# LayerNorm mean of the Conformer module taken from the convolved tiles in PSUM, squares summed by pairs

## The chip, the cores and the metric

The kernel runs on one core of a Trainium2 chip. The metric is the device time of one execution in microseconds (us), from the runs of the same program on the chip.

## What is computed

The reference is one inference step of a two-layer trunk for 512 prompt tokens and 8 sequences of 8 sample tokens (576 token columns in the kernel). Layer 0 is a Mamba-2/S5 mixer and an MLP, layer 1 a Conformer convolution module and an MLP. The change lies in the convolution module:

```python
def conformer_conv_module(xn, buf, w_pw1, b_pw1, w_dw, b_dw, ln_w, ln_b, w_pw2, b_pw2):
    h = xn @ w_pw1 + b_pw1
    h = h[..., :C_CH] * jax.nn.sigmoid(h[..., C_CH:])
    h, new_buf = causal_depthwise_conv(h, buf, w_dw, b_dw)
    h = jax.nn.silu(layer_norm(h, ln_w, ln_b))
    return h @ w_pw2 + b_pw2, new_buf
```

There are 1024 channels and 31 taps; `layer_norm` subtracts the mean over the channels and divides by the root of the mean square of what is left.

## The kernel before

Activations lie with channels on the 128 partitions and the 576 token columns in the free dimension, so 1024 channels are eight tiles, m = 0 to 7. A dense layer is `mm` (L226): the weights are split in `load` into a high and a low part (ScalarE writes `hi`, L211; VectorE writes `lo`, L212), and each output tile takes 48 matmuls of 288 columns. Two PSUM buffers named `mm` alternate.

`conformer` loops over m. In each turn two `mm` calls give the gate (`cs`) and the value (`ct`), VectorE takes both out of PSUM (L1167) and multiplies them into `hb`, the convolution's input with 30 columns of history in front (L1189). `dwconv` of tile m-1 is written one turn later. It works in one of three ways:

- Tiles in the list `PT` go through `dwconv_pe`: a ScalarE copy (`hp`), a write to DRAM and four reads back in another order (`hq`), 36 matmul calls (72 instructions) with prepared weights `dm` (L1308), a ScalarE copy (`ho`), four writes and a read (`hy`), and a ScalarE pass with the bias into `acc` (L1317).
- Tiles with `ND` = 30 take their first tap on ScalarE and 30 taps on VectorE, one instruction of 512 columns each (L1376).
- Tile 7 is split: `ND[7]` taps on VectorE, the rest on TensorE against diagonal weights, three matmuls of 512 columns a tap (L1374), added by L1380.

The sample columns of each tile add eight small VectorE instructions (L1341).

The LayerNorm's mean is not taken from the results. `tap_sums` (L1259) multiplies each `hb` by its 31 tap weights and sums over channels in two PSUM banks (`pt`). After tile 7 `neg_mean` copies them to SBUF (`pz`), writes them to DRAM (`pzd`), reads them back with each tap's row shifted by its tap (`pk`), and sums the rows with a matmul against -1/1024 (`mu`, L1282); a ScalarE copy gives `nmu` (L1283). Biases and sample histories are centred ahead of time by `dwconv_center` in the first MLP. Tile 7's prompt columns get the mean through a matmul into their own bank (L1363); tiles 0 to 6 get it by a VectorE addition (L1208). Then ScalarE squares each tile (L1211) and ten one-column matmul instructions a tile sum the squares over channels (L1216), 80 in all. `rstd_tok`, `bcast_tok`, a VectorE product and a Silu on ScalarE lead to the second dense layer `w_pw2`, again `mm`.

The order on each engine is set by a scheduler with a cost model, by program order and by the offsets `HP` and `HPC`. Each engine then works through its list in that order. All DMAs named here are issued on SyncE's queue.

Of the kernel before, what the change touches and what calls it, by code (L numbers as in the profile page):

```python
# [8 lines left out]
F32 = mybir.dt.float32  # L9
# [129 lines left out]
def h2(t):  # L139
    return t.rearrange("p (h n) -> p h n", h=2)  # L140


class Build:
# [182 lines left out]
    def _ffn(self, i, x):  # L326
# [33 lines left out]
        for q in range(4):  # L360
            if q == 3 and i == 1:
                for n in range(16):
                    down_half(n % 8, g, n // 8)
                    if n == 9 or n == 15:
                        self.final(x, n // 15)
                break
            gn = []
            for m in range(8):
                if q < 3:
                    gn.append(up(q * 8 + 8 + m))  # L370
                if q == 1 and i == 0:
                    self.dwconv_state(self.qp, m)
                    if m == 7:
                        self.dwconv_center()
                if q == 0 and i == 0:
                    self.ssm_state(self.qp, m)
                down(q, m, g)
            g = gn
# [773 lines left out]

    ND = [0, 30, 0, 0, 30, 0, 30, 14]

    NEV = 1
    ORD = [0, 1, 2, 3, 4, 5, 6, 7]
    SQ = "aaaaaaaa"
# [10 lines left out]

    PT = [0, 2, 3, 5]
    NDM = 5  # L1170

    def conformer(self, x):
        nc, I = self.nc, self.I
        with self.tc.tile_pool(name="q2", bufs=2) as q:
            act = [self.split_scaled(x[k], self.v("nm1", k), "fx", self.B) for k in range(8)]
            _, rB = self.rms(x, "rB1")
            acc, hbs = [], []
            ps31 = [self.bank("pt0"), self.bank("pt1", "sf")]
            for m in range(8):
                ps = self.mm(I["w_pw1"][8 + m], act)  # L1180
                s = self.t("cs", "t")
                self.evac(s, ps, rB, m < self.NEV)
                nc.scalar.activation(s, s, AF.Sigmoid, bias=self.v("bpw1", 8 + m))
                ps = self.mm(I["w_pw1"][m], act)
                t = self.t("ct", "t2")
# [8 lines left out]
                if m in self.PT:  # L1194
                    for g in range(4):
                        self.dwconv_mat(q, m, g)
                with self.hp(self.HP if m == 7 else 0):
                    self.tap_sums(q, m, hb, ps31)
                if m > 0:
                    self.dwconv(q, m - 1, hbs[m - 1], acc[m - 1])  # L1200
            nmu = self.neg_mean(q, ps31)
            self.dwconv(q, 7, hbs[7], acc[7], nmu)
            nmu = nmu[0]

            ts = self.bank("tsum")
            for n, k in enumerate(self.ORD):
                if k < 7:
                    nc.vector.tensor_tensor(acc[k], acc[k], nmu, op=ALU.add)  # L1208
                s = self.B("sq")
                if self.SQ[n] == "a":  # L1210
                    nc.scalar.activation(s, acc[k], AF.Square)  # L1211
                else:
                    nc.vector.tensor_tensor(s, acc[k], acc[k], op=ALU.mult)
                for c in (0, 4, 1, 2, 3):
                    m = min(128, NT - c * 128)
                    nc.tensor.matmul(ts[:m, c:c + 1], s[:, c * 128:c * 128 + m], self.ones[:, 0:1], start=n + c == 0, stop=(n, c) == (7, 3))  # L1216
            r = self.tp.tile([128, 5], F32, tag="r5", name="r5")
# [11 lines left out]
    def dwconv_init(self, q):  # L1229

        nc = self.nc
        self.wdh = q.tile([128, 248], F32R, tag="wdh", name="wdh")
        self.wdl = q.tile([128, 248], F32, tag="wdl", name="wdl")
        nc.scalar.activation(self.wdh, self.v("dww", 0, 248), AF.Copy)
        nc.vector.tensor_tensor(self.wdl, self.v("dww", 0, 248), self.wdh.bitcast(F32), op=ALU.subtract)
        self.ss = q.tile([128, 8, 64], F32, tag="ss", name="ss")
        self.bdc = q.tile([128, 8], F32, tag="bdc", name="bdc")
        self.neg = q.tile([128, 128], F32, tag="neg", name="neg")
        nc.gpsimd.memset(self.neg, -1.0 / 1024)
        self.pzd = self.dp.tile([31, 670], F32, tag="pzd", name="pzd")  # L1240
        tiles = lambda n, s: {m: self.dp.tile(s, F32, tag="%s%d" % (n, m), name="%s%d" % (n, m)) for m in self.PT}
        self.dd, self.de = tiles("dd", [128, 4, 136]), tiles("de", [128, 4, 128])
        self.dm = {}

    def dwconv_center(self):

        nc = self.nc
        s = self.tp.tile([128, NT], F32, tag="sa", name="s1", bufs=1)
        nc.vector.tensor_reduce(s[:, 0:64], self.ss.rearrange("p m t -> p t m"), axis=mybir.AxisListType.X, op=ALU.add)
        nc.vector.tensor_reduce(s[:, 64:65], self.v("bdw", 0, 8), axis=mybir.AxisListType.X, op=ALU.add)  # L1250
        ps = self.bank("cm")
        nc.tensor.matmul(ps[:, 0:65], self.neg, s[:, 0:65], start=True, stop=True)
        nc.vector.tensor_tensor(self.ss, self.ss, ps[:, 0:64].unsqueeze(1).broadcast_to([128, 8, 64]), op=ALU.add)
        nc.vector.tensor_tensor(self.bdc, self.v("bdw", 0, 8), ps[:, 64:65].broadcast_to([128, 8]), op=ALU.add)

    def tap_sums(self, q, m, hb, ps):

        for h in range(2):
            self.nc.tensor.matmul(ps[h][:31, 0:H], self.v("dww", m * 31, 31), hb[:, 30 + h * H:30 + h * H + H], start=m == 0, stop=m == 7)  # L1259

    def neg_mean(self, q, ps):

        nc = self.nc
        pz = q.tile([31, 670], F32, tag="pz", name="pz", bufs=1)
        pk = q.tile([31, NT], F32, tag="pk", name="pk", bufs=1)
        nc.gpsimd.memset(pz[:, 0:30], 0.0)
        nc.gpsimd.memset(pz[:, 542:670], 0.0)
        nc.gpsimd.memset(pk[:, NP:NT], 0.0)
        out = q.tile([128, NT], F32, tag="nmu", name="nmu", bufs=1)
        with self.hp():  # L1270
            nc.scalar.activation(pz[:, 30:30 + H], ps[0][:31, 0:H], AF.Copy)
            nc.scalar.activation(pz[:, 30 + H:542], ps[1][:31, 0:NP - H], AF.Copy)
            nc.scalar.activation(pz[:, 542:670].rearrange("p (b j) -> p b j", b=8)[:, :, 8:16],
                                 ps[1][:31, NP - H:H].rearrange("p (b j) -> p b j", b=8), AF.Copy)
            nc.sync.dma_start(self.pzd, pz)
            nc.scalar.activation(q.tile([31, 1], F32, tag="ld", name="ld", bufs=1), pz[:, 31:32], AF.Silu)
            d = self.pzd
            nc.sync.dma_start(pk[23:31, NP:NT], bass.AP(tensor=d.tensor, offset=d.offset + 23 * 671 + 520, ap=[[671, 8], [16, 8], [1, 8]]))
            nc.sync.dma_start(pk[:, 0:NP], bass.AP(tensor=d.tensor, offset=d.offset, ap=[[671, 31], [1, NP]]))
            mu = self.pm.tile([128, 2, 512], F32, tag="mm", name="mu")[:, :, :H]  # L1280
            for h, o, n in ((0, 0, H), (1, 0, NP - H), (1, NP - H, 64)):
                nc.tensor.matmul(mu[:, h, o:o + n], self.neg[:31], pk[:, h * H + o:h * H + o + n], start=True, stop=True)  # L1282
            nc.scalar.activation(h2(out), mu, AF.Copy)  # L1283
        return out, pk

# [6 lines left out]
    def dwconv_pe(self, q, m, hb, a):  # L1292
# [18 lines left out]
        with self.hp(self.HPC):  # L1311
# [4 lines left out]
            nc.sync.dma_start(y, self.de[m])  # L1316
            nc.scalar.activation(a[:, 0:NP].rearrange("p (n f) -> p f n", f=4), y, AF.Identity, bias=self.bdc[:, m:m + 1])  # L1317

# [13 lines left out]

    def dwconv(self, q, m, hb, a, nmu=None):

# [4 lines left out]
        for d in range(8):  # L1339
            src = an if d else self.ss[:, m].rearrange("p (b t) -> p b t", b=8)  # L1340
            nc.vector.scalar_tensor_tensor(an[:, :, d:8], hn[:, :, 0:8 - d], self.v("dww", m * 31 + 30 - d), src[:, :, d:8],  # L1341
                                           op0=ALU.mult, op1=ALU.add)
        if nmu is not None:
            nc.vector.tensor_tensor(a[:, NP:], a[:, NP:], nmu[0][:, NP:], op=ALU.add)
        if m in self.PT:
# [5 lines left out]
        k0 = 1 + self.ND[m]  # L1351
        nc.scalar.activation(ap, hb[:, 0:NP], AF.Identity, scale=w(0), bias=self.bdc[:, m:m + 1])
        pc = None
        if k0 < 31:
# [5 lines left out]
            pc = self.bank("pc", "sd" if m % 2 else "sf")  # L1360
            if nmu is not None:
                with self.hp(self.HPC):
                    nc.tensor.matmul(pc, self.neg[:31], nmu[1][:, 0:NP], start=True, stop=False)  # L1363
            for k in range(k0, 31, 4):
# [7 lines left out]
                for j in range(n):  # L1372
                    for i, (dd, h) in enumerate(((dh, hh), (dh, hl), (dl, hh))):
                        nc.tensor.matmul(pc, dd[:, j], h[:, k + j:k + j + NP], start=k + j == k0 and i == 0 and nmu is None, stop=k + j == 30 and i == 2)  # L1374
        for k in range(1, k0):
            nc.vector.scalar_tensor_tensor(ap, hb[:, k:k + NP], w(k), ap, op0=ALU.mult, op1=ALU.add)  # L1376
        if pc is None and nmu is not None:
            nc.vector.tensor_tensor(ap, ap, nmu[0][:, 0:NP], op=ALU.add)
        if pc is not None:
# [39 lines left out]
```

## Time and profile before

| | us |
|---|---|
| median of three runs | 1678.6 (1676.21 to 1682.48) |
| the profiled execution | 1674.24 |
| its span, first to last instruction | 1672.5 |
| TensorE busy | 1591.3 |
| VectorE busy | 1054.5 |
| ScalarE busy | 634.8 |

A profile page gives the busy time of each engine, a strip of 40 equal slices of the span, and the chain of work that ended last. In the strip a digit is the busy share of a slice in tenths; the line PEclk shows the clock that TensorE was granted, in tenths of full speed. Each slice is 41.8 us. In lists of the trace L numbers are lines of the kernel, PEld is TensorE's weight load, `out<-in` names the tiles, and xN says how many instructions a row holds.

### The profile page before, as it was taken

To read this page: it belongs to the slowest core of one execution; us is meant where nothing else is said; L and a number is where in the kernel's file an instruction comes from. 1 tells how busy PE (TensorE), PEld (TensorE's weight loads), DVE (VectorE), ACT (ScalarE), POOL (GpSimd) and SP (SyncE) were. 2 spreads that over 40 slices of the span, in tenths; PEclk is the share of its full clock that TensorE was granted. 3 is DMA by queue.
4 is the path that set the end of the run, shared out by engine and by line. 5 is a ranking of instruction groups with operands and counts; after the bars stand their busy time and mean duration, and the time that the engine had idled before them with its cause. 6 is when DMAs were issued, how large, how long until landed. Compare 5 with 4: busy or idle time off the path is not lost.

```text
span 1672.5 us, 28815 instructions
## 1 busy us (share of the span) xinstructions
PE 1591.3 (95%) x11833; PEld 1557.6 (93%) x11833; DVE 1054.5 (63%) x1796; ACT 634.8 (38%) x1081; POOL 4.7 (0%) x45
## 2 busy tenths in 40 slices
PE   7999889999998999999999999996799999999997
PEld 7999789989897999999999999995799999999996
DVE  7988899876647966754443557587454443444466
ACT  4244556675514333322222353223333222222244
POOL 0000000000000000000000000000000000000000
PEclk9999999999998999999999999997799999999998
DMA  6644457687766434432222245641022222222234
GB/s 197 180 109 132 131 172 197 197 267 220 251 234 188 94 97 129 154 127 78 87 77 88 78 146 148 189 107 30 25 77 77 89 76 89 85 81 88 78 127 132
DMA packets 149883, 214.43 MB, mean 128 GB/s; under 512 B 59034, under 2 KB 94874, under 8 KB 149752
## 3 DMA queue, kind: packets, MB, share of 16 engines
q1 hardware_dynamic: 146088, 211.28, 41.2%
q8 instruction: 93, 1.52, 0.4%
q10 hardware_dynamic: 3664, 1.32, 0.3%
q14 instruction: 38, 0.31, 0.1%
HBM read 181.22 MB, written 31.34 MB: 127 GB/s over the span
## 4 chain that ended last, share of the span: by engine, by line
PE 82%; DVE 7%; DMA 6%; ACT 2%; issue 1%; SPq 1%; ACTq 0%; DVEq 0%
PE mm L226 72%; PE pc L1308 2%; DVE lo L212 1%; DMA sg<-cumd 1%; DMA rl<-yad 1%; PE pc L1374 1%; PE tsum L1216 1%; PE bc L310 1%; DMA rl<-ybd 1%; DMA rl<-yg 1%; PE pt L1259 1%; DMA ud<-u 1%; PE s5s L600 1%; PE s5y L704 0%; PE s5y L705 0%
## 5 line engine op out<-in xcount | busy, mean ns | idle before, releaser
L211 ACT ACTIVATE hi<-raw 128x1024 fp32r<-128x1024 f32 x217 | 229.7, 1060 | 740.2 <-PE mm L226 685.6
L226 PE MATMUL mm<-fxh,hi 128*128 128x288 f32 x1920 | 418.2, 299 | 23.8 <-ACT hi L211 10.4
L212 DVE TENSOR_TENSOR lo<-raw,hi 128x1024 fp32r<-128x1024 f32 x217 | 264.8, 1221 | 259.0 <-ACT hi L211 257.5
L226 PE MATMUL mm<-fxh,lo 128*128 128x288 f32 x1920 | 417.4, 298 | 0.0
L226 PE MATMUL mm<-fxl,hi 128*128 128x288 f32 x1920 | 415.0, 298 | 0.0
L226 PEld LDWEIGHTS mm<-fxh,hi 128*128 128x128 f32 x1920 | 311.7, 190 | 26.7 <-ACT hi L211 12.7
L226 PEld LDWEIGHTS mm<-fxh,lo 128*128 128x128 f32 x1920 | 311.6, 190 | 1.8 <-issue 1.1
L226 PEld LDWEIGHTS mm<-fxl,hi 128*128 128x128 f32 x1920 | 311.9, 190 | 0.4
L226 PE MATMUL mm<-gh,hi 128*128 128x288 f32 x1024 | 230.0, 295 | 0.0
L226 PE MATMUL mm<-gh,lo 128*128 128x288 f32 x1024 | 229.4, 295 | 0.5 <-DVE lo L212 0.5
L226 PE MATMUL mm<-gl,hi 128*128 128x288 f32 x1024 | 229.5, 295 | 0.0
L226 PEld LDWEIGHTS mm<-gh,lo 128*128 128x128 f32 x1024 | 167.5, 188 | 0.8 <-DVE lo L212 0.8
L226 PEld LDWEIGHTS mm<-gl,hi 128*128 128x128 f32 x1024 | 167.9, 188 | 0.0
L226 PEld LDWEIGHTS mm<-gh,hi 128*128 128x128 f32 x1024 | 167.6, 188 | 0.0
L350 DVE TENSOR_TENSOR fft<-mm,r2B 128x576 f32<-128x576 f32 x56 | 42.4, 758 | 140.5 <-PE mm L226 140.5
L1376 DVE SCALAR_TENSOR_TENSOR acc<-hb,vec,acc 128x512 f32<-128x512 f32 x104 | 77.2, 748 | 1.3
L343 DVE TENSOR_TENSOR ffr<-ffr 128x576 f32<-128x576 f32 x64 | 48.5, 758 | 2.3 <-ACT gh L342 0.4
L344 DVE TENSOR_TENSOR gl<-ffr,gh 128x576 fp32r<-128x576 f32 x64 | 48.5, 758 | 2.1
L342 ACT ACTIVATE gh<-ffr 128x576 fp32r<-128x576 f32 x64 | 44.1, 689 | 2.0
L351 DVE TENSOR_TENSOR x<-x,fft 128x576 f32<-128x576 f32 x56 | 42.4, 758 | 1.8
L765 DVE SCALAR_TENSOR_TENSOR cvo<-xb,vh,cvo 128x600 f32<-128x600 f32 x48 | 40.0, 833 | 1.4 <-ACT cvo L763 1.4
L340 ACT ACTIVATE ffr<-mm 128x576 f32<-128x576 f32 x64 | 40.6, 634 | 0.0
(356 smaller groups left out, 1903.1 us busy)
## 6 DMA issues: line engine op xcount, KB each, us to landing
raw<-w_ff SPq DMA_DIRECT2D x136, 512.0 KB, 3.5
raw<-w_in SPq DMA_DIRECT2D x33, 512.0 KB, 3.7
raw<-w_pw SPq DMA_DIRECT2D x24, 512.0 KB, 3.6
dm<-dwm SPq DMA_DIRECT2D x16, 576.0 KB, 5.9
h<-ass SPq DMA_DIRECT2D x16, 512.0 KB, 4.7
raw<-w_out SPq DMA_DIRECT2D x16, 512.0 KB, 4.5
U<-ud SPq DMA_DIRECT2D x16, 288.0 KB, 3.0
xsd<-xs SPq DMA_DIRECT2D x16, 288.0 KB, 4.0
```

The lines of the kernel that those rows point to most:

```text
L211: nc.scalar.activation(hi, raw, AF.Copy)
L212: eng.tensor_tensor(lo, raw, hi.bitcast(F32), op=ALU.subtract)
L226: nc.tensor.matmul(ps[:, h, :H], w[:, k], a[:, h * H:(h + 1) * H], start=n == 0, stop=n == 23)
L340: nc.scalar.activation(h2(r), ps, AF.Relu)
L342: nc.scalar.activation(hi, r, AF.Square)
L343: nc.vector.tensor_tensor(r, r, r, op=ALU.mult)
L344: nc.vector.tensor_tensor(lo, r, hi.bitcast(F32), op=ALU.subtract)
L350: nc.vector.tensor_tensor(h2(t), ps, rB, op=ALU.mult)
L351: nc.vector.tensor_tensor(x[m], x[m], t, op=ALU.add)
L765: nc.vector.scalar_tensor_tensor(o[:, 0:600], xb[:, k:k + 600], self.half("acw", 16 * k + m), o[:, 0:600], op0=ALU.mult, op1=ALU.add)
L1308: nc.tensor.matmul(pc[:, g * 128:g * 128 + 128], w[:, j * 128:j * 128 + 128], hq[:, g, j:j + 128], start=j == 0, stop=j == 8)
L1376: nc.vector.scalar_tensor_tensor(ap, hb[:, k:k + NP], w(k), ap, op0=ALU.mult, op1=ALU.add)
```

## The change

The mean is now computed from the convolved tiles themselves: `mean` multiplies each `acc` by a 128 x 128 matrix of -1/1024 and accumulates over the eight tiles in the two banks `mu`, which hold the negative mean for every column on every partition. `tap_sums`, `neg_mean` with its DRAM passage, `dwconv_center` and the centred biases `bdc` go; the plain bias is used. Two ScalarE copies of 288 columns give `nmu`. All eight tiles then get the mean on VectorE. The squares are added two by two on VectorE, and one group of matmuls serves a pair, 40 instructions in place of 80. `PT` becomes 0, 2, 4, 6, tiles 1, 3 and 5 take 30 taps on VectorE, and tile 7 takes 20 on VectorE and 10 on TensorE (before 14 and 16). The instruction that makes ScalarE load its Silu table early moves up behind the last gate.

```diff
@@ ffn
-                    if m == 7:
-                        self.dwconv_center()
@@
-    ND = [0, 30, 0, 0, 30, 0, 30, 14]
+    ND = [0, 30, 0, 30, 0, 30, 0, 20]
-    ORD = [0, 1, 2, 3, 4, 5, 6, 7]
+    ORD = [0, 1, 2, 3, 4, 5, 7, 6]
-    PT = [0, 2, 3, 5]
+    PT = [0, 2, 4, 6]
@@ conformer
-            ps31 = [self.bank("pt0"), self.bank("pt1", "sf")]
+            mu = [self.bank("mu0"), self.bank("mu1", "sf")]
+            done = []
+                if m == 7:
+                    nc.scalar.activation(q.tile([128, 1], F32, tag="ld", name="ld", bufs=1), s[:, 0:1], AF.Silu)
-                with self.hp(self.HP if m == 7 else 0):
-                    self.tap_sums(q, m, hb, ps31)
                 if m > 0:
                     self.dwconv(q, m - 1, hbs[m - 1], acc[m - 1])
-            nmu = self.neg_mean(q, ps31)
-            self.dwconv(q, 7, hbs[7], acc[7], nmu)
-            nmu = nmu[0]
+                if m > 1 and m - 2 not in self.PT:
+                    self.mean(mu, acc, m - 2, done)
+                if m > 3 and m - 4 in self.PT:
+                    self.mean(mu, acc, m - 4, done)
+            self.dwconv(q, 7, hbs[7], acc[7])
+            for m in self.ORD:
+                if m not in done:
+                    self.mean(mu, acc, m, done)
+            nmu = q.tile([128, NT], F32, tag="nmu", name="nmu", bufs=1)
+            for h in range(2):
+                nc.scalar.activation(nmu[:, h * H:h * H + H], mu[h][:, 0:H], AF.Copy)
...
-                if k < 7:
-                    nc.vector.tensor_tensor(acc[k], acc[k], nmu, op=ALU.add)
-                s = self.B("sq")
+                nc.vector.tensor_tensor(acc[k], acc[k], nmu, op=ALU.add)
+                sq = self.B("sq")
+                nc.scalar.activation(sq, acc[k], AF.Square)
+                if n % 2 == 0:
+                    s = sq
+                    continue
+                nc.vector.tensor_tensor(s, s, sq, op=ALU.add)
@@
+    def mean(self, mu, acc, m, done):
         for h in range(2):
+            self.nc.tensor.matmul(mu[h][:, 0:H], self.neg, acc[m][:, h * H:h * H + H], start=not done, stop=len(done) == 7)
+        done.append(m)
@@ dwconv
-        if nmu is not None:
-            nc.vector.tensor_tensor(a[:, NP:], a[:, NP:], nmu[0][:, NP:], op=ALU.add)
-            if nmu is not None:
-                with self.hp(self.HPC):
-                    nc.tensor.matmul(pc, self.neg[:31], nmu[1][:, 0:NP], start=True, stop=False)
```

TensorE in the middle of the loop, behind the eighth of the sixteen dense output tiles. Before, the tap sums of tile 3 (`pt`) stand inside the convolution of tile 2 (`pc`):

```order
L226 MATMUL mm<-fxh,lo 128x288 x2
L1308 MATMUL pc<-hq,dm 128x128 x18
L1259 MATMUL pt_10964<-hb,vec 31x288
L1259 MATMUL pt_10965<-hb,vec 31x288
L1308 MATMUL pc<-hq,dm 128x128 x18
L226 MATMUL mm<-fxh,hi 128x288 x2
```

and at that point of the new list:

```order
L226 MATMUL mm<-fxl,hi 128x288 x2
L1278 MATMUL pc<-hq,dm 128x128 x36
L1253 MATMUL mu_10955<-acc,neg 128x288
L1253 MATMUL mu_10956<-acc,neg 128x288
L226 MATMUL mm<-fxh,lo 128x288 x2
```

The mean's first pair, for tile 1, now stands there between dense matmuls, and it reads `acc`, not `hb`. The next pair that reads taps of VectorE, tile 3's, stands in the same way right behind the 36 calls of tile 4's convolution. On VectorE the last tap of tile 1 stands two taps behind `hb` of tile 3, and the last tap of tile 3 is the first one behind `hb` of tile 5.

TensorE at the end of the loop, from the last dense matmul of `w_pw1` on. Before:

```order
L226 MATMUL mm<-fxh,lo 128x288 x2
L1259 MATMUL pt_10964<-hb,vec 31x288
L1259 MATMUL pt_10965<-hb,vec 31x288
L1282 MATMUL mu<-pk,neg 128x288
L1282 MATMUL mu<-pk,neg 128x224
L1282 MATMUL mu<-pk,neg 128x64
L1363 MATMUL pc<-pk,neg 128x512
L1374 MATMUL pc<-hh,dh 128x512
```

Now the convolution of a whole `PT` tile, tile 6, stands behind the last dense matmul, then the mean of tile 5 and tile 7's diagonal taps (30 rows, of which the first stands here):

```order
L226 MATMUL mm<-fxh,lo 128x288 x2
L1278 MATMUL pc<-hq,dm 128x128 x36
L1253 MATMUL mu_10955<-acc,neg 128x288
L1253 MATMUL mu_10956<-acc,neg 128x288
L1339 MATMUL pc<-hh,dh 128x512
```

Behind those taps three more pairs of L1253 follow, for tiles 4, 7 and 6, and then the sums of squares. So five tiles' means stand ahead of tile 7's taps, four of them inside the loop (tiles 1, 0, 3, 2), and three behind.

VectorE at the end of the stage, ahead of the reciprocal root (L290). Before, the additions of the mean stand among the last taps of tiles 6 and 7:

```order
L1208 TENSOR_TENSOR acc<-acc,nmu 128x576
L1341 SCALAR_TENSOR_TENSOR acc<-hb,vec,acc 128x8x2
L1208 TENSOR_TENSOR acc<-acc,nmu 128x576 x5
L1376 SCALAR_TENSOR_TENSOR acc<-hb,vec,acc 128x512 x2
L1341 SCALAR_TENSOR_TENSOR acc<-hb,vec,acc 128x8
L1376 SCALAR_TENSOR_TENSOR acc<-hb,vec,acc 128x512 x2
L1344 TENSOR_TENSOR acc<-acc,nmu 128x64
L1376 SCALAR_TENSOR_TENSOR acc<-hb,vec,acc 128x512
L1208 TENSOR_TENSOR acc<-acc,nmu 128x576
L1376 SCALAR_TENSOR_TENSOR acc<-hb,vec,acc 128x512 x6
L1380 TENSOR_TENSOR acc<-acc,pc 128x512
L290 TENSOR_SCALAR rv<-tsum 128x4
```

Now all taps come first, then the eight additions, then the four pair sums:

```order
L1311 SCALAR_TENSOR_TENSOR acc<-hb,vec,acc 128x8
L1341 SCALAR_TENSOR_TENSOR acc<-hb,vec,acc 128x512 x14
L1343 TENSOR_TENSOR acc<-acc,pc 128x512
L1214 TENSOR_TENSOR acc<-acc,nmu 128x576 x8
L1220 TENSOR_TENSOR sq<-sq 128x576 x4
L290 TENSOR_SCALAR rv<-tsum 128x4
```

Between `hb` of tile 7 and this piece VectorE has one tap of tile 5, six of tile 7's 20, the split of `hb` for TensorE (`hl`) and the eight small instructions of tile 7. 89 of the 110 taps stand ahead of `hb` of tile 7 (before 81 of 104).

## Rows read from the trace of the kernel before

**Rows 1.** The page: busy time of each engine, and the strip of TensorE's clock.
```profile
PE 1591.3 (95%) x11833; PEld 1557.6 (93%) x11833; DVE 1054.5 (63%) x1796; ACT 634.8 (38%) x1081; POOL 4.7 (0%) x45
...
PEclk9999999999998999999999999997799999999998
```

**Rows 2.** Stretches: us, then busy us (instructions) of PE, PEld, DVE, ACT, POOL; PEclk.
```profile
1010.80:1138.50 127.70, 124.41 (x943) 118.00 (x941) 101.34 (x176) 35.79 (x38) 0.42 (x4) 1.00 0.50 142
1138.50:1192.80 54.30, 34.94 (x150) 28.37 (x150) 31.10 (x65) 17.96 (x33) 0.00 (x0) 0.63 0.06 14
```

**Rows 3.** Chain of work that ended last, 1137 to 1193 us: start, length, what.
```profile
1137.84 0.74 DVE hb L1189
...
1140.96 5.51 DMA pzd<-pz
...
1146.83 4.21 DMA pk<-pzd
...
1151.17 2.36 PE mu L1282 x6
1153.53 1.81 PE pc L1363 x2
1155.34 13.24 PE pc L1374 x48
1168.58 13.03 PE tsum L1216 x80
...
1192.83 37.26 PE mm L226 x264
```

**Rows 4.** The same chain in the loop: dense matmuls, one `PT` tile, one tile's tap sums.
```profile
1086.39 19.18 PE mm L226 x144
...
1113.10 4.02 PE pc L1308 x36
1117.12 1.09 PE pt L1259 x4
1118.21 4.21 PE pc L1308 x36
```

**Rows 5.** TensorE in order of time: start, length; the last dense matmuls of `w_pw1`.
```profile
1134.78 0.43 PE L226 MATMUL mm<-fxh,lo 128*128 128x288 f32 x2
```

**Rows 6.** VectorE in order of time: `hb` of tile 5, taps, `hl`, additions.
```profile
1102.88 0.81 DVE L1189 SCALAR_TENSOR_TENSOR hb<-ct,vec,cs 128x576 f32<-128x576 f32 x1
...
1116.92 0.74 DVE L1376 SCALAR_TENSOR_TENSOR acc<-hb,vec,acc 128x512 f32<-128x512 f32 x1
...
1117.76 0.75 DVE L1376 SCALAR_TENSOR_TENSOR acc<-hb,vec,acc 128x512 f32<-128x512 f32 x1
...
1140.01 0.72 DVE L1359 TENSOR_TENSOR hl<-hb,hh 128x542 fp32r<-128x542 f32 x1
...
1155.07 3.43 DVE L1208 TENSOR_TENSOR acc<-acc,nmu 128x576 f32<-128x576 f32 x5
...
1162.68 4.68 DVE L1376 SCALAR_TENSOR_TENSOR acc<-hb,vec,acc 128x512 f32<-128x512 f32 x6
1168.62 0.69 DVE L1380 TENSOR_TENSOR acc<-acc,pc 128x512 f32<-128x512 f32 x1 [1.26 <-PE pc L1374]
```

**Rows 7.** ScalarE in order of time: tile 5's return from DRAM, the copy `nmu`.
```profile
1128.99 1.25 ACT L1317 ACTIVATE acc<-hy,bdc 128x512 f32<-128x512 f32 x1 [5.93 <-DMA hy<-de]
...
1153.57 0.65 ACT L1283 ACTIVATE nmu<-mu 128x576 f32<-128x576 f32 x1 [11.11 <-PE mu L1282]
```

**Rows 8.** Stretches of 2 us, columns as in rows 2: the clock.
```profile
1136.00:1138.00 2.00, 0.00 (x0) 0.00 (x0) 2.00 (x4) 0.09 (x1) 0.00 (x0) 1.00 0.00 0
1138.00:1140.00 2.00, 1.38 (x4) 0.42 (x4) 2.00 (x4) 1.40 (x3) 0.00 (x0) 0.74 0.49 109
...
1170.00:1172.00 2.00, 2.00 (x19) 1.96 (x19) 0.00 (x0) 0.03 (x1) 0.00 (x0) 1.00 0.00 0
...
1176.00:1178.00 2.00, 2.00 (x11) 1.99 (x10) 0.00 (x0) 0.00 (x0) 0.00 (x0) 0.50 0.00 0
```

More of the change, by code (lines that the diff above doesn't have):

```diff
@@ L1196, in conformer @@
                         self.dwconv_mat(q, m, g)
-                with self.hp(self.HP if m == 7 else 0):
-                    self.tap_sums(q, m, hb, ps31)
                 if m > 0:
                     self.dwconv(q, m - 1, hbs[m - 1], acc[m - 1])
-            nmu = self.neg_mean(q, ps31)
-            self.dwconv(q, 7, hbs[7], acc[7], nmu)
-            nmu = nmu[0]
+                if m > 1 and m - 2 not in self.PT:
[9 more added lines that the diff above has]
+                nc.scalar.activation(nmu[:, h * H:h * H + H], mu[h][:, 0:H], AF.Copy)
             ts = self.bank("tsum")
             for n, k in enumerate(self.ORD):
-                if k < 7:
-                    nc.vector.tensor_tensor(acc[k], acc[k], nmu, op=ALU.add)
-                s = self.B("sq")
[L1210 to L1213, printed above, removed]
+                nc.vector.tensor_tensor(acc[k], acc[k], nmu, op=ALU.add)
[5 more added lines that the diff above has]
+                nc.vector.tensor_tensor(s, s, sq, op=ALU.add)
                 for c in (0, 4, 1, 2, 3):
                     m = min(128, NT - c * 128)
-                    nc.tensor.matmul(ts[:m, c:c + 1], s[:, c * 128:c * 128 + m], self.ones[:, 0:1], start=n + c == 0, stop=(n, c) == (7, 3))
+                    nc.tensor.matmul(ts[:m, c:c + 1], s[:, c * 128:c * 128 + m], self.ones[:, 0:1], start=n + c == 1, stop=(n, c) == (7, 3))
             r = self.tp.tile([128, 5], F32, tag="r5", name="r5")
@@ L1236, in dwconv_init @@
         self.ss = q.tile([128, 8, 64], F32, tag="ss", name="ss")
-        self.bdc = q.tile([128, 8], F32, tag="bdc", name="bdc")
         self.neg = q.tile([128, 128], F32, tag="neg", name="neg")
         nc.gpsimd.memset(self.neg, -1.0 / 1024)
-        self.pzd = self.dp.tile([31, 670], F32, tag="pzd", name="pzd")
         tiles = lambda n, s: {m: self.dp.tile(s, F32, tag="%s%d" % (n, m), name="%s%d" % (n, m)) for m in self.PT}
@@ L1243, in dwconv_init @@
         self.dm = {}
[L1245 to L1254, printed above, removed]
@@ L1256, in tap_sums @@
-    def tap_sums(self, q, m, hb, ps):
-        for h in range(2):
[L1259 to L1284, printed above, removed]
@@ L1316, in dwconv_pe @@
             nc.sync.dma_start(y, self.de[m])
-            nc.scalar.activation(a[:, 0:NP].rearrange("p (n f) -> p f n", f=4), y, AF.Identity, bias=self.bdc[:, m:m + 1])
+            nc.scalar.activation(a[:, 0:NP].rearrange("p (n f) -> p f n", f=4), y, AF.Identity, bias=self.v("bdw", m))
     def dwconv_state(self, q, m):
@@ L1331, in dwconv_state, with dwconv @@
         nc.vector.tensor_scalar(self.ss[:, m], self.ss[:, m], self.v("bdw", m), None, op0=ALU.add)
-    def dwconv(self, q, m, hb, a, nmu=None):
+    def dwconv(self, q, m, hb, a):
         nc = self.nc
@@ L1351, in dwconv @@
         k0 = 1 + self.ND[m]
-        nc.scalar.activation(ap, hb[:, 0:NP], AF.Identity, scale=w(0), bias=self.bdc[:, m:m + 1])
+        nc.scalar.activation(ap, hb[:, 0:NP], AF.Identity, scale=w(0), bias=self.v("bdw", m))
         pc = None
@@ L1373, in dwconv @@
                     for i, (dd, h) in enumerate(((dh, hh), (dh, hl), (dl, hh))):
-                        nc.tensor.matmul(pc, dd[:, j], h[:, k + j:k + j + NP], start=k + j == k0 and i == 0 and nmu is None, stop=k + j == 30 and i == 2)
+                        nc.tensor.matmul(pc, dd[:, j], h[:, k + j:k + j + NP], start=k + j == k0 and i == 0, stop=k + j == 30 and i == 2)
         for k in range(1, k0):
             nc.vector.scalar_tensor_tensor(ap, hb[:, k:k + NP], w(k), ap, op0=ALU.mult, op1=ALU.add)
-        if pc is None and nmu is not None:
-            nc.vector.tensor_tensor(ap, ap, nmu[0][:, 0:NP], op=ALU.add)
         if pc is not None:
```

## The prediction

> **What bounds the kernel now.** I read the page first. TensorE is busy for 95% of the span, and its clock stands at nine tenths or more nearly everywhere; the one pair of sevens in the middle of the strip is the place of this change [rows 1]. Next I asked for two stretches around it. From 1010.8 to 1138.5 us, the loop over tiles, TensorE is busy 124.4 of 127.7 us and VectorE 101.3, so VectorE has 26.4 us to spare. From there to the first matmul of `w_pw2`, 54.3 us, TensorE is busy 34.9 us at a mean clock of 0.63 [rows 2]. Then the chain of waits, which names what ends last in that stretch [rows 3]: `hb` of tile 7, a write to DRAM of 5.5 us, a read of 4.2, the sum `mu` of 2.4, 1.8 us to put the mean into tile 7's bank, 13.2 us of tile 7's diagonal taps, 13.0 us of sums of squares, and 11.2 us (from 1181.6 to 1192.8) of reciprocal root, broadcast and Silu. TensorE sets the end of the loop, the passage of the mean through DRAM and the matmuls behind it set the tail. I go by the profiled execution (1674.24 us, span 1672.5), where `w_pw2` starts at 1192.83, and move that start; behind it nothing is changed.
>
> **The loop.** The last dense matmul of `w_pw1` ends at 1135.2 [rows 5]. A `PT` tile costs TensorE 4.02 + 4.21 = 8.2 us, a tile's tap sums 1.09 us [rows 4]. Ahead of that last matmul stood four `PT` tiles and seven tap sums; now three and four means. A mean is the same number of instructions over the same 576 columns, only with 128 output rows in place of 31; for the same columns the `PT` matmuls give 576/128 x 2 x 4.02/36 = 1.0 us, so I take 1.09. The sum is -8.2 - 7 x 1.09 + 4 x 1.09 = -11.5, and the last dense matmul ends at 1123.7. From it to the end of `hb` of tile 7 (1138.6) was 3.4 us [rows 3, 5]; the same four VectorE instructions stand there, so `hb` comes at 1127.1.
>
> This holds if VectorE keeps up. Ahead of that `hb` it has eight more taps, 8 x 0.75 = 6 us [rows 6]: 107.3 us of work in 1010.8 to 1127.1, 116.3 us. Nine are left. The `PT` tiles now alternate with VectorE's tiles, which spreads them. Tile 6's columns must be back from DRAM when TensorE gets to them: for tile 5 that took from 1103.7 to 1113.1 at most, 9.4 us [rows 4, 6], and now two dense tiles and a mean (2 x 6.4 + 1.1, by 19.18 us for 144 matmuls [rows 4]) less 3.4 leave 10.5. No wait there, by a narrow margin. `dwconv_center`, some 2 us of VectorE in the first MLP with two short matmuls, costs nothing gone, since TensorE carries that stage. The early Silu table sits on ScalarE, busy 35.8 of 127.7 us [rows 2], and costs nothing either.
>
> **The new wait.** TensorE works its list in order, so a mean in the loop holds up all dense matmuls behind it until its `acc` is done, and through them VectorE's next `hb`. Tiles 0 and 2 came back long before. Tile 1's last taps stand behind `hb` of tile 3 and its mean behind 8.2 us of convolution: 8.2 - 3.4 - two taps and two small instructions of 0.84 a pair = 3 us of margin; tile 3's mean has 8.2 - 3.4 - 0.75 = 4. I cost them at nothing; without that cover they cost their wait in full, on the path.
>
> **From `hb` to tile 7's sums.** VectorE: one tap 0.67, a small instruction 0.2, `hl` 0.7 and another 0.2, six pairs of tap and small instruction at 0.84 (1116.92 to 1117.76), one small 0.15, and 14 taps on the same `acc` at 0.785 (4.68 us for six) = 11.0; then the addition of the bank, 0.69 [rows 6]. Together 18.6 us, so tile 7 is done at 1145.7, against 1169.3 before. TensorE meanwhile does tile 6 (8.2), tile 5's mean, 30 diagonal matmuls (13.24/48 = 0.28 each [rows 3], part of them at half clock, so no less than the price here) and tile 4's mean: 1123.7 + 8.2 + 1.1 + 8.3 + 1.1 = 1142.4, ahead of tile 7's end. Tile 6's `acc` took 7.8 us behind its last matmul (1122.4 to 1130.2 for tile 5 [rows 4, 7]): 1139.7, also ahead.
>
> **The mean, exposed.** Means of tiles 7 and 6 remain behind tile 7's addition. TensorE will have stood some 3 us; before, it stood from 1135.2 to 1138.6, and its clock was full at 1136 to 1138 and 0.74 over 1138 to 1140 [rows 8]. Nearest to that, I take half clock: 1.81 us for 512 columns at that clock [rows 3] makes 2.04 for 576, twice 4.1 (at full clock 2.2; by `mu`'s 2.36 a tile 4.7). 1149.8. The second `nmu` copy is half of 0.65 and some start, 0.4 [rows 7]: 1150.2. The new wait on VectorE has the eight additions queued behind it and nothing else.
>
> **Additions and squares.** Eight additions at 0.67 (3.43 us for five [rows 6]) and the first pair sum: 7 x 0.67 + 0.76 + 0.76 = 6.2, so the first group of sums starts at 1156.4; ScalarE's squares run alongside. The other pair sums take 0.67 each and stay ahead of TensorE. 40 instructions: the 80 before ran 19 in 2 us at clock 1.00 and 11 at 0.50 [rows 8], 0.105 and 0.18 us each. TensorE will have stood 6 us, so 40 x 0.18 = 7.2 (full clock: 4.2), to 1163.6. Then 11.2 as before: `w_pw2` starts at 1174.8, 18.0 us earlier. Of these the loop gives 11.5; the tail from `hb` to `w_pw2` shrinks from 54.2 to 47.7 us and gives 6.5, about the six by which the sums of squares are shorter: six more taps on VectorE and two exposed means take most of what the passage through DRAM leaves.
>
> The Trainium skill, page "TensorE: Matmul & The Clock Gate", section "LDWEIGHTS (loading the stationary operand)", gives a weight load about P/1.2 ns for P columns and names no clock. By it 128 columns take 107 ns, and 40 would take some 4.3 us; this trace has that pace at clock 1.00 and not at 0.50, so the sum goes by the row.
>
> **The sum.** Span 1672.5 - 18.0 = 1654.5, the execution 1656.2. The profiled execution lies 4.4 us under the median of the runs shown, 1678.6; on that basis 1660.6.
>
> **Rivals.** *The loop does not get shorter* (the change does not do there what its order says): VectorE, not TensorE, paces it, keeps the 26 us it idled [rows 2], and `hb` of tile 7 stays at 1138.6 as the moved convolution only leaves TensorE waiting. For it: margins of 1 to 4 us. Against it: nine spare microseconds and a TensorE that hardly stood in the loop. The tail alone is then 18.6 + 29.1 = 47.7 against 54.2, a gain of 6.5: 1672.
>
> *The in-loop means dam the matmul queue*: tile 1's and tile 3's means each wait for `acc`, the dense matmuls stand behind them, VectorE then starves and makes the next `acc` later. For it: the order shows both waits, with 3 and 4 us of margin. Against it: VectorE's surplus. It turns the sign when the two waits add up to over 18 us; at 13.5 us each it is 1660.6 + 27 = 1688. The same rule stands in the Trainium skill, page "PSUM — Partial Sum Buffer", section "Engine vs sequencer instructions": matmuls start and complete in program order. The trace agrees as far as it goes: tile 7's taps, whose `hl` was ready at 1140.7, ran only behind `mu` and the mean at 1155.3 [rows 3, 6].
>
> *The clock holds in the tail*: if the gap behind tile 4's mean is shorter or the clock slower to fall, the means take 2.2 and the sums 4.2: 1.9 + 3.0 less, 1655.7. Against it: the half clock of most of the stretch before.
>
> **How the numbers follow.** My forecast 0.66, its own range 1656 to 1667 (tile 7 up to 5 us late, or the clock half won). Loop no shorter 0.18, dam 0.07, clock held 0.09. Run to run the kernel moves by 3 us either way. 1653 to 1673 leaves out the dam, some of the loop case and the edge of the clock case, under 0.2. 0.5% is 8.4 us, about what a measurement of this kernel can tell from no change. Faster by more: the forecast, the clock and a third of the loop case, 0.81; within it 0.13; slower 0.06, nearly all of the dam.
>
> **What would show it.** The last dense matmul of `w_pw1` near 1124 and `hb` of tile 7 within 4 us of it (the loop); no idle time of TensorE ahead of the in-loop means (the dam); tile 7's addition some 18.6 us behind its `hb`; two means at about 2 us each, then ten-instruction groups at 0.18 an instruction; 29 us from the addition to `w_pw2`. I am wrong if TensorE shows waits for `acc` in the loop, if tile 6's columns come late and TensorE stands at full length behind the last dense matmul, or if `w_pw2` begins later than 1184.

## The result, and the profile after

| | kernel before | changed kernel |
|---|---|---|
| median of four runs each, taken together (us) | 1680.54 (1676.21 to 1683.55) | 1664.38 (1658.83 to 1667.97) |
| profiled execution (us) | 1674.24 | 1663.62 |
| its span (us) | 1672.5 | 1661.8 |

The ratio is 0.9895, with a 95% interval of 0.9863 to 0.9926: 16.2 us less, where 18.0 were forecast. A second comparison, further down, gave 0.9898 (0.9878 to 0.9918).

The page of the changed kernel, against [rows 1]: TensorE has 10.6 us less to do, VectorE 5.3 us more, and of the two sevens in the strip of the clock one has become an eight. Two eights stand further left, in layer 0, where the kernel before had one.

```profile
PE 1580.7 (95%) x11765; PEld 1553.0 (93%) x11765; DVE 1059.8 (64%) x1802; ACT 629.9 (38%) x1067; POOL 4.4 (0%) x42
...
PEclk9999998989999999999999999998799999999998
```

The two spans differ by 10.7 us only. The chain of work says why. I call the *stage* the time from the first dense matmul behind the broadcast `bc` (`w_pw1`) to the first of `w_pw2`. In the kernel before it begins so:

```profile
1009.14 1.25 PE bc L310 x10
1010.39 7.79 PE mm L226 x57
```

and in the changed kernel so (start, length, what):

```profile
1013.91 1.25 PE bc L310 x10
1015.16 7.14 PE mm L226 x52
```

Everything ahead of this, layer 0, which the change does not touch except for the small `dwconv_center`, ran 4.77 us longer in the execution that was profiled, and what lies behind the start of `w_pw2` 1.27 us longer. The stage itself went from 1192.83 - 1010.39 = 182.4 to 165.7 us, 16.7 less: 16.7 - 4.8 - 1.3 = 10.7. Single executions of one kernel differ by a few microseconds in layer 0: in a second profile of the changed kernel (e9_after) `w_pw1` began at 1012.43 us instead of 1015.16. So the experiments below are compared by the stage of their profile, and by time only where they were timed in rounds. Each has one profile; the two of the changed kernel gave stages of 165.7 and 165.0 us, so a difference of 0.7 us or less between stages is within the variation.

The chain in the stage of the changed kernel, against [rows 3] and [rows 4]:

```profile
1091.94 8.04 PE pc L1278 x72
1099.98 0.97 PE mu L1253 x4
1100.95 10.28 PE mm L226 x78
...
1111.26 1.23 DVE lo L212
...
1118.76 0.73 DVE hb L1190
...
1131.05 0.73 DVE hb L1190
...
1149.43 0.70 DVE acc L1343
...
1150.17 4.22 PE mu L1253 x8
...
1154.42 0.42 ACT nmu L1210
...
1155.54 4.76 DVE acc L1214 x7
1160.30 0.68 DVE sq L1220
...
1161.02 8.55 PE tsum L1223 x40
...
1180.86 51.25 PE mm L226 x368
```

On this chain no DMA stands behind `hb` of tile 7 any more. In its place VectorE's taps fill the 17.7 us from the end of `hb` (1131.78) to the start of tile 7's addition (L1343), and then come the means that are left over, the additions and the sums. From 1111 us on the chain runs over VectorE: VectorE, no longer TensorE, ends the loop, though TensorE is still busy for 115.11 of its 116.13 us. The stretches, against [rows 2] (us, then busy us of PE, PEld, DVE, ACT, POOL; clock), show how little is left of VectorE's 26 us: 116.13 - 105.38 = 10.8.

```profile
1015.57:1131.70 116.13, 115.11 (x889) 113.86 (x888) 105.38 (x184) 35.40 (x38) 0.41 (x4) 1.00 0.53 151
1131.70:1180.86 49.16, 29.18 (x140) 24.81 (x138) 33.76 (x68) 15.28 (x23) 0.00 (x0) 0.70 0.10 23
```

TensorE's waits in the stage (us in total, times, longest): the only mean that waits for an `acc` is the one behind tile 7's addition.

```profile
PE tsum L1223 <- DVE sq L1220: 6.6, 1, 6.6
...
PE mu L1253 <- DVE acc L1343: 4.7, 1, 4.7
...
PE pc L1278 <- DMA hq<-dd: 1.0, 2, 0.8
```

### The profile page after: what moved, and what is told of

Its sections match the earlier page's. It is cut to its first block, busy times and chain, and to the rows that moved or that the text cites. A ratio compares the mean times of both kernels' runs of the same rounds, so it can differ in the third digit from the quotient of the medians.

```text
span 1661.8 us, 28663 instructions
## 1 busy us (share of the span) xinstructions
PE 1580.7 (95%) x11765; PEld 1553.0 (93%) x11765; DVE 1059.8 (64%) x1802; ACT 629.9 (38%) x1067; POOL 4.4 (0%) x42
## 3 DMA queue, kind: packets, MB, share of 16 engines
q8 instruction: 92, 1.51, 0.4%
## 4 chain that ended last, share of the span: by engine, by line
PE 79%; DVE 10%; DMA 7%; ACT 1%; issue 1%; SPq 1%; ACTq 0%; DVEq 0%
PE mm L226 71%; DVE acc L1341 2%; PE pc L1278 1%; DVE lo L212 1%; DMA rl<-ybd 1%; PE yoff L964 1%; PE s5y L702 1%; PE bc L310 1%; PE s5y L703 1%; DMA sg<-cumd 1%; DMA rl<-yg 1%; DMA ud<-u 1%; DMA h<-ass 1%; PE tsum L1223 1%; DMA bt<-btd 1%
## 5 line engine op out<-in xcount | busy, mean ns | idle before, releaser
L1341 DVE SCALAR_TENSOR_TENSOR acc<-hb,vec,acc 128x512 f32<-128x512 f32 x110 | 82.5, 750 | 1.5
```

## The experiments

No kernel here leaves out a part of the computation; e8_clock adds matmuls whose result nothing reads. "Tail" is the time from the end of `hb` of tile 7 to `w_pw2`; the loop is given by the end of that `hb`, counted from the start of `bc`.

| kernel | stage | loop | tail |
|---|---|---|---|
| before | 182.4 | 129.6 | 54.3 |
| e1_tiles_only | 177.8 | 121.6 | 57.7 |
| e2_mean_only | 171.6 | 126.8 | 46.3 |
| e4_pairs_only | 175.4 | 129.6 | 47.3 |
| changed | 165.7 | 118.0 | 49.1 |
| e3_no_pairs | 168.2 | 118.0 | 51.6 |
| e5_mean6_first | 163.8 | 118.1 | 47.2 |
| e6_nd18 | 161.5 | 118.4 | 44.5 |
| e7_quads | 159.6 | 117.9 | 43.0 |
| e8_clock | 159.6 | 118.0 | 43.0 |

### The choice of tiles alone, on the kernel before (e1_tiles_only)

```diff
-    ND = [0, 30, 0, 0, 30, 0, 30, 14]
+    ND = [0, 30, 0, 30, 0, 30, 0, 14]
-    PT = [0, 2, 3, 5]
+    PT = [0, 2, 4, 6]
```

> The kernel before with one edit: the tiles are dealt out as after the change (PT 0, 2, 4, 6; tiles 1, 3, 5 on VectorE; tile 7 stays at 14 and 16 taps); the mean still goes through DRAM and 80 instructions sum the squares. Measure: the stage from the first dense matmul behind the broadcast rB1 to the first matmul of w_pw2, 182.4 us before and 165.7 after. Theory A (the dealing takes one tile's convolution, 8.2 us, out of the loop, the rest of the loop's gain is tap sums; the tail is another matter): hb of tile 7 comes about 8 us earlier, the tail stays at 54 to 55, the stage is 174 to 176. Rival B (the gain is the DRAM passage going, the dealing only makes room): the stage stays at 181 to 183.

The loop lost 8.0 us, the price of one `PT` tile in [rows 4], but the stage only 4.6: neither theory's figure. The rest went back in the tail, which is 3.4 us longer. TensorE in order of time:

```profile
1133.43 4.18 PE L1308 MATMUL pc<-hq,dm 128*128 128x128 f32 x36
1137.54 1.16 PE L1259 MATMUL pt<-hb,vec 128*31 128x288 f32 x4
1138.63 4.29 PE L1308 MATMUL pc<-hq,dm 128*128 128x128 f32 x36
```

`hb` of tile 7 ended at 1135.3, but the sums of its taps stand between the two halves of tile 6's convolution and ran at 1137.54, so they ended 3.4 us behind `hb` (1.9 before). The Trainium skill, page "PSUM — Partial Sum Buffer", section "Engine vs sequencer instructions", says that matmuls start and complete in program order; the rows agree, since the tap sums had their input at 1135.3 and began within 0.1 us of the end of the half tile in front of them. On ScalarE a second thing stands in the way. In the kernel before, its load of the Silu table began when the copies to `pz` were done:

```profile
1140.95 1.28 ACT L1276 ACT_TABLE_LOAD   x1
```

In e1 the load and the small instruction `ld` that brings it (both L1276) stand between the first copy and the other two. The chain:

```profile
1138.25 0.40 ACT pz L1271
...
1138.67 0.12 ACT L1276
...
1139.96 0.20 ACT ld L1276
1140.16 0.24 ACT pz L1272
1140.40 0.12 ACT pz L1273
...
1140.53 5.51 DMA pzd<-pz
```

So the write `pzd` began 5.2 us behind `hb` (2.4 before): of the 2.8 us, 1.5 come from the matmuls in front of the tap sums and 1.3 from ScalarE's list. That is a DRAM passage held up by what stands ahead of its start, on two engines. On top of the new mean, without that passage, the tiles gain 8.8 us in the loop and the tail gives 2.8 back (e2 against the changed kernel, which also differ in the split of tile 7 and the order of the sums).

### The mean and the pairs, with the old tiles (e2_mean_only)

```diff
-    ND = [0, 30, 0, 30, 0, 30, 0, 20]
+    ND = [0, 30, 0, 0, 30, 0, 30, 14]
-    ORD = [0, 1, 2, 3, 4, 5, 7, 6]
+    ORD = [0, 1, 2, 3, 4, 5, 6, 7]
-    PT = [0, 2, 4, 6]
+    PT = [0, 2, 3, 5]
```

> The changed kernel with the tiles dealt as before (PT 0, 2, 3, 5; tiles 1, 4, 6 on VectorE; tile 7 at 14 and 16), mean from the accumulated tiles, squares by pairs. Theory A: the loop gains only the three tap sums that no mean replaces, about 3 us; behind hb of tile 7 stand 22 taps of tiles 6 and 7 on VectorE, 18 us, then the same 30.7 us as after the change: a tail of 49 and a stage of 173 to 175. Rival B (DRAM passage is the whole gain): the stage is within 2 us of 165.7. With e1 it also says whether the two parts add up: 7 to 8 and 8 to 9 of 16.7.

The diff is against the changed kernel. The loop lost 2.8 us, as expected: seven tap sums went, four means came. The tail came out shorter than expected, 46.3, and with it the stage, 171.6; the row of the exposed mean shows the reason:

```profile
1150.65 1.51 PE L1253 MATMUL mu<-acc,neg 128*128 128x288 f32 x4 [2.45 <-DVE acc L1343]
1158.80 8.53 PE L1223 MATMUL tsum<-ones,sq 128*128 128x1 f32 x40 [6.64 <-DVE sq L1220]
```

Only one mean stood behind tile 7's addition, since tile 6's was issued ahead of it, and it took 1.51 us, not 2 x 2.1. The changed kernel sums tile 7 before tile 6 (`ORD` ends in 7, 6), so tile 6's mean waits behind tile 7's although its `acc` is done earlier. On ScalarE tile 6 came back in the changed kernel at 1144.27, 5.9 us ahead of tile 7's addition:

```profile
1143.04 1.23 ACT L1287 ACTIVATE acc<-hy,vec 128x512 f32<-128x512 f32 x1 [5.83 <-DMA hy<-de]
```

e1 and e2 together gain 4.6 + 10.8 = 15.4 of the 16.7 us; on top of the new mean the tiles, with the split of tile 7 and the order of the sums, are worth 5.9. The split at 20 taps and the earlier Silu table were not tried alone.

### Without pairs, and pairs alone (e3_no_pairs, e4_pairs_only)

e3 is the changed kernel with 80 instructions for the sums:

```diff
-                if n % 2 == 0:
-                    s = sq
-                    continue
-                nc.vector.tensor_tensor(s, s, sq, op=ALU.add)
+                s = sq
...
```

> The changed kernel without the pairing: every tile's squares go to TensorE, 80 instructions. Theory A: the sums start about 4.7 us earlier, behind the first square, but run at 0.21 us each at half clock, 17.1 us: 3.9 us later at their end, stage 169 to 170. Rival C (the instructions count in full): 40 x 0.21 = 8.5 us, stage 174. Rival D (the pair sums on VectorE cost what they save): stage 165 to 166.

e4 is the kernel before with the pairs:

```diff
-                s = self.B("sq")
-                if self.SQ[n] == "a":
-                    nc.scalar.activation(s, acc[k], AF.Square)
-                else:
-                    nc.vector.tensor_tensor(s, acc[k], acc[k], op=ALU.mult)
+                sq = self.B("sq")
+                nc.scalar.activation(sq, acc[k], AF.Square)
+                if n % 2 == 0:
+                    s = sq
+                    continue
+                nc.vector.tensor_tensor(s, s, sq, op=ALU.add)
...
```

> The kernel before with the pairing alone. Theory A: three of the four groups are ready when tile 7's taps end on TensorE, the last 1.5 us behind; 40 instructions end 5 to 7 us earlier than the 80: stage 175.5 to 177.5. Rival D: no gain, 181 to 183, since the pair sums on VectorE stand among the last taps and make tile 7 late.

The pairs are worth 2.5 us in the changed kernel, less than the 3.9 expected, and 7.0 on the kernel before, the most that was expected. The sums of e3 and, below it, those of e4:

```profile
1153.18 16.09 PE L1220 MATMUL tsum<-ones,sq 128*128 128x1 f32 x80 [2.01 <-ACT sq L1216]
```

```profile
1164.47 3.62 PE L1217 MATMUL tsum<-ones,sq 128*128 128x1 f32 x30
1168.44 2.26 PE L1217 MATMUL tsum<-ones,sq 128*128 128x1 f32 x10 [0.35 <-DVE sq L1214]
```

In e3 the 80 last 7.5 us longer than the 40, but they begin with the first square, 1.6 us behind `nmu` instead of 6.2, and run beside the additions: 7.5 - 4.6 = 2.9, less 0.3 by which the means were cheaper in this run. In e4, 30 of the 40 run at 0.12 us each beside VectorE's last taps of tile 7, where the mean of tiles 0 to 5 has already been added, and only ten stand behind the last pair sum; tile 7's addition begins 31.5 us behind `hb` instead of 30.1, as three pair sums now stand among VectorE's taps and the mean came 0.6 us later in this run. What pairing saves on the path is thus not "40 instructions fewer" but the difference of what is left when the last square is ready.

### The order of the last means, and the split of tile 7 (e5_mean6_first, e6_nd18)

```diff
-            for m in self.ORD:
+            for m in (4, 6, 7):
```

> The changed kernel with one edit: the mean of tile 6 stands ahead of that of tile 7, so that one mean, not two, waits for tile 7's addition. The stage is from the first dense matmul behind the broadcast rB1 to the first matmul of w_pw2: 165.7 us after the change. Theory A: tile 6 came back 6 us ahead of tile 7's addition, so its mean moves into TensorE's idle time; one mean stays exposed, 1.5 to 2.0 us in place of 4.2: stage 163 to 163.6. Rival B (the order of the two costs nothing, the clock alone sets 4.2): 165 to 166.

```diff
-    ND = [0, 30, 0, 30, 0, 30, 0, 20]
+    ND = [0, 30, 0, 30, 0, 30, 0, 18]
```

(on top of e5)

> As e5, and tile 7 at 18 taps on VectorE and 12 on TensorE (after the change 20 and 10). Theory A: VectorE's chain of dependent taps sets tile 7's end, so two taps fewer give 1.6 us; TensorE's six more matmuls, 1.4 us, fill its idle time, which then is under 1 us, so the exposed mean runs at full clock, 1.1 us. Stage 161 to 162. Rival B (TensorE becomes the bound, since its taps and two means now end with VectorE's chain): no better than e5, 163 to 164.

Tile 6's mean ahead of tile 7's gave 1.9 us, a little less than expected, since the exposed mean took 2.29 us and not 1.5 to 2.0. Two taps moved from VectorE to TensorE gave 2.35 more, as expected: 2 x 0.785 for the taps and 1.05 because the exposed mean got cheaper, less 0.3 in the loop, which is within the variation between profiles. e5 and, below it, e6:

```profile
1144.95 2.10 PE L1253 MATMUL mu<-acc,neg 128*128 128x288 f32 x8
1150.67 2.29 PE L1253 MATMUL mu<-acc,neg 128*128 128x288 f32 x4 [3.62 <-DVE acc L1343]
```

```profile
1149.86 2.10 PE L1253 MATMUL mu<-acc,neg 128*128 128x288 f32 x8
1153.36 1.24 PE L1253 MATMUL mu<-acc,neg 128*128 128x288 f32 x4 [1.39 <-DVE acc L1343]
```

With 3.62 us of standing in front, the four instructions took 2.29 us; with 1.39 us, 1.24.

### Squares by fours (e7_quads), and matmuls to keep the clock (e8_clock)

On top of e6, 20 instructions for the sums:

```diff
-                if n % 2 == 0:
+                if n % 4 == 0:
                     s = sq
                     continue
                 nc.vector.tensor_tensor(s, s, sq, op=ALU.add)
+                if n % 4 < 3:
+                    continue
...
```

> As e6, and the squares are added by fours on VectorE: two groups, 20 instructions, in place of 40. Theory A: from nmu to the end of the sums 14.7 us became, with eight additions, six sums and one group of ten at 0.21, 11.6 to 12: 3 us less, stage 158 to 159. Rival B (VectorE's sums now stand on the path in full, so nothing is won): 161 to 162, as e6.

The stage fell by 1.9 us, less than expected: the sums last 4.36 in place of 8.54 us, 4.2 less, but start 8.9 us behind `nmu` instead of 6.2. That makes 1.5 us of tail; the other 0.4 lie in the loop, which the edit does not touch.

On top of e7, one matmul of 288 columns behind each addition, into a bank that nothing reads:

```diff
+            jk = self.bank("jk", "sf")
...
                 nc.scalar.activation(sq, acc[k], AF.Square)
+                nc.tensor.matmul(jk[:, 0:H], self.neg, acc[k][:, 0:H], start=True, stop=True)
```

> As e7, and behind each addition of the mean one matmul of 288 columns of that tile against the constant matrix goes to a spare PSUM bank, whose content nobody reads: TensorE works while VectorE adds. It measures the price of the half clock in the tail. Theory A: the clock stays full through the sums and the broadcast, 10 instructions behind the last sum take 1.1 in place of 2.1 us and the broadcast 1.25 in place of 2.1: stage 1.5 to 2 us under e7. Rival B (one-column matmuls take the clock down at once, whatever stood ahead): same as e7. Rival C (the extra matmuls stand in the way of the sums): 1 us or more above e7.

The same 159.6, the figure of rival B, but not for the reason that rival B gives. The matmuls held the clock while they ran, TensorE then stood 2.59 us, and the sums ran at half clock all the same. TensorE in order of time, and the stretches of 2 us (columns as in [rows 8]):

```profile
1145.03 5.34 PE L1218 MATMUL jk<-acc,neg 128*128 128x288 f32 x16 [1.38 <-DVE acc L1215]
1152.96 4.34 PE L1227 MATMUL tsum<-ones,sq 128*128 128x1 f32 x20 [2.59 <-DVE sq L1222]
```

```profile
1150.00:1152.00 2.00, 0.37 (x2) 0.00 (x0) 2.00 (x4) 0.34 (x1) 0.00 (x0) 1.00 0.00 0
1152.00:1154.00 2.00, 1.04 (x5) 1.01 (x6) 1.58 (x3) 0.00 (x0) 0.00 (x0) 0.75 0.00 0
1154.00:1156.00 2.00, 2.00 (x11) 1.97 (x11) 0.00 (x0) 0.00 (x0) 0.00 (x0) 0.50 0.00 0
```

In the kernel before, matmuls do run right up to the sums, which begin at 1168.42, and there the clock stays up at first: 1.00 from 1170 to 1172 us [rows 8], then

```profile
1172.00:1174.00 2.00, 2.00 (x16) 1.94 (x15) 0.00 (x0) 0.00 (x0) 0.00 (x0) 0.78 0.00 0
1174.00:1176.00 2.00, 2.00 (x11) 1.97 (x11) 0.00 (x0) 0.00 (x0) 0.00 (x0) 0.50 0.00 0
```

In e4, too, the 30 sums that follow tile 7's matmuls ran at 1.00 up to 1168 us. So one-column matmuls do not take the clock down at once. In e8 it fell near 1153, after the 2.59 us in which TensorE stood; that these were the reason is likely but not shown, as matmuls right up to the sums were not tried on e7.

### The version of e7, timed in rounds (e9_best, e9_after)

> The kernel of e7_quads again, timed in rounds. Theory A: its stage stands at 159.6 us as in e7_quads, 22.9 us under the kernel before and 6.1 us under the changed kernel, and nothing elsewhere pays for it: the ratio to the kernel before is 1 - 22.9 / 1680 = 0.986, between 0.984 and 0.989. Rival B: something outside the stage gives part of it back, or the variation of layer 0 between executions is as large as the step: the ratio stands at 0.990 or above, where the changed kernel is.

> The changed kernel again, on the same chip as e9_best. Theory A: ratio to the kernel before 1 - 16.7 / 1680 = 0.990, some 0.004 above that of e9_best. Rival B: no difference from e9_best that the interval can tell.

On one chip, beside 1676.54 us for the kernel before (11 runs): e7's version 1654.13 us (1652.52 to 1659.44, 4 runs), ratio 0.9864 (0.9843 to 0.9886); the changed kernel 1660.31 us (1656.18 to 1664.02, 6 runs), ratio 0.9898 (0.9878 to 0.9918). Their stages are 159.3 and 165.0 us. The medians lie 6.2 us apart and the stages 5.7, as theory A has it, but the two intervals overlap, so the step of about a third of a per cent rests more on the stages than on the times. The order of the last means, two taps and the sums by fours belong on this kernel.

## Why the prediction was right, and where it was not

| step | predicted (us) | measured (us) |
|---|---|---|
| `hb` of tile 7 earlier by | 11.5 | 11.55 |
| from it to the end of tile 7's addition | 18.6 | 18.33 |
| two exposed means | 4.1 | 4.21 |
| second `nmu` copy | 0.4 | 0.42 |
| additions and first pair sum | 6.2 | 6.1 |
| 40 instructions of sums | 7.2 | 8.54 |
| from there to `w_pw2` | 11.2 | 11.3 |
| tail | 47.7 | 49.1 |
| gain | 18.0 | 16.7 |

**The loop** was right, and e1 (8.0) and e2 (2.8) show its two parts each by itself, 10.8 of the 11.55 us together. Two small errors cancel in it: means at 0.97 and `PT` tiles at 8.04 us let the last dense matmul end 12.5 us earlier, not 11.5, and `hb` then came 4.3 us behind it, not 3.4, as VectorE had become the last. The margin at tile 6's columns was overestimated in the same way: `hb` of tile 6 ended 5.8 us behind the tile's last matmul, not 3.4, and TensorE waited 0.8 us where none was forecast:

```profile
1128.29 8.28 PE L1278 MATMUL pc<-hq,dm 128*128 128x128 f32 x72 [0.80 <-DMA hq<-dd]
```

It cost nothing, since tile 7's taps on VectorE ended later than TensorE's work. The dam did not come: no in-loop mean waited for its `acc`.

**The term that failed** is that of the sums, 8.54 us where 7.2 were forecast. 0.18 us an instruction came from eleven instructions in a stretch of 2 us [rows 8]. That count includes the instructions cut by the stretch's two edges. The changed kernel shows the same count, while the group as a whole gives 8.54 / 40 = 0.214 us:

```profile
1161.02 8.54 PE L1223 MATMUL tsum<-ones,sq 128*128 128x1 f32 x40 [6.64 <-DVE sq L1220]
```

```profile
1164.00:1166.00 2.00, 2.00 (x11) 1.99 (x10) 0.00 (x0) 0.00 (x0) 0.00 (x0) 0.50 0.00 0
```

The 1.3 us of difference are as large as the whole error of the gain; each other term is off by 0.3 us or less. The page of the Trainium skill that the prediction weighed there, "TensorE: Matmul & The Clock Gate", section "LDWEIGHTS (loading the stationary operand)", gives P/1.2 ns for P columns, about 107 ns for 128, which makes 4.3 us by estimate, or 3.8 since eight of the 40 instructions load 64 columns: the row measures twice that and more at clock 0.50, and the 30 sums of e4, at 0.12 us each and clock 1.00, come near it.

**An attribution held in one order only.** The prediction put about six of the tail's 6.5 us down to the shorter sums. Added to the kernel before, the pairs do give 7.0 us (e4). Taken out of the changed kernel they cost 2.5 us of the 5.2 measured (e3), and the other 2.7 are what is left of the gain from the DRAM passage. What a part is worth depends on what else is in place. The number was close since it was a sum over the new path, in which the attribution had no part.

**The clock** came out as forecast for the means and the sums, and the case in which it holds did not come. For the means this was in part luck. TensorE stood from 1145.5 to 1150.2, 4.7 us and not some 3, because `hb` came 4.3 us behind the dense matmuls and not 3.4, and tile 7's 30 matmuls took 7.2 us and not 8.3. A mean cost 1.51 us behind 2.45 us of standing (e2) and 2.29 behind 3.62 (e5), so behind 3 us the price was open. For the sums, the clock rose behind the means and fell again before they began, which was not foreseen:

```profile
1146.00:1148.00 2.00, 0.00 (x0) 0.00 (x0) 1.89 (x4) 0.00 (x0) 0.00 (x0) 0.94 0.00 0
1148.00:1150.00 2.00, 0.00 (x0) 0.00 (x0) 1.86 (x3) 0.00 (x0) 0.00 (x0) 0.50 0.00 0
...
1154.00:1156.00 2.00, 0.38 (x1) 0.00 (x0) 1.14 (x2) 0.76 (x2) 0.00 (x0) 0.86 0.00 0
1156.00:1158.00 2.00, 0.00 (x0) 0.00 (x0) 2.00 (x4) 2.00 (x4) 0.00 (x0) 1.00 0.00 0
1158.00:1160.00 2.00, 0.00 (x0) 0.00 (x0) 2.00 (x4) 2.00 (x4) 0.00 (x0) 0.50 0.00 0
```

## What to carry to other kernels

Price a step by the duration of a whole group of its instructions, not by their count in a short stretch, which includes those that its edges cut. When work is halved, ask what of it stands behind the last input: the same pairing gave 7.0 us where the early part ran under other work and 2.5 where it began later for it. In a queue that runs in order, put the part whose input comes first ahead of the one that comes last (1.9 us here), and look at what stands ahead of a DRAM passage's start on every engine that feeds it (2.8 us in e1).

## What the runs showed of the hardware that was not expected

- TensorE's clock rose to full level while TensorE did nothing: in the rows above it stood at 1.00 from 1156 to 1158 us, behind two means at half clock, and was at 0.50 again at 1158 with no matmul in between. In e5, behind one mean at half clock, it stayed at 0.50 until the sums began.
- Sums of one-column matmuls kept TensorE listed as busy without a gap (2.00 of 2.00 us) at a clock of 0.50 from 1162 to 1168 us in the changed kernel, and from 1154 to 1156 us in e8. In the kernel before they began at 1.00 and fell to 0.50 by 1174 us, also without a gap.
- Four mean instructions behind a standing TensorE took 1.24 us after 0.68, 0.80 and 1.39 us (e8, e7, e6), with the clock at 1.00; 1.51 after 2.45 (e2), where it fell to 0.50 meanwhile; and 2.29 after 3.62 (e5), where it fell as they began. Right behind other matmuls they took 1.13 (changed kernel, at 1144.34, in the same view). The waits of e2 and e5 were thus paid twice, in the wait and in the matmuls behind it; those of e6 to e8 cost 0.1 us there.
